# Moving normalisation, a branch and several sums of a stick-breaking / convolution layer between stages and queues

## The chip, the cores and the metric

The kernel runs on one core of a Trainium2 chip. The core has a matrix engine (PE, with its weight loads shown apart as PEld), a vector engine (DVE), an activation engine (ACT), a general engine (POOL) and a queue engine (SP); transfers run on 16 DMA engines. Each engine works through its own instructions in order. The metric is the device time of the program in microseconds (us).

## What is computed

The input is x, 2048 positions of 1024 numbers. After a layer normalisation one product with `w_in` gives nine blocks; two branches follow and are merged:

```python
h = layer_norm(x) @ w_in                     # q k v z_sb c_val c_gate z_cv g_sb g_cv
o_sb = stick_breaking_attention(q, k, v)     # 16 heads of 64
y_sb = (o_sb * silu(z_sb)) @ w_sb_proj
u = causal_depthwise_conv(c_val * sigmoid(c_gate))        # 31 taps
u = silu(layer_norm(u, conv_ln_g, conv_ln_b))
y_cv = (u * silu(z_cv)) @ w_cv_proj
merged = sigmoid(g_sb) * y_sb + sigmoid(g_cv) * y_cv
out = layer_norm(2 ** 0.25 * layer_norm(x) + merged @ w_out)
# attention, s < t: weight(t, s) = sigmoid(l_ts) * prod over s < j < t of (1 - sigmoid(l_tj))
```

Everything is in 32-bit floating point.

## The kernel before

**Numbers split in two.** A matrix operand is kept as a high part `hi` (a rounded copy, made on ACT) and a low part `lo = src - hi` (DVE); a product is three matmuls, hi x hi, hi x lo, lo x hi. `split` (lines 115 to 117) does this, for activations, weights and attention weights alike. So L116 is ACT and L117 is DVE wherever something is split.

**Tiles and stages.** The positions run backwards in memory and are cut in four chunks of 512; chunks 3 and 2 form half h = 1, chunks 1 and 0 half h = 0. Channels are eight blocks of 128. What is needed later goes to DRAM tiles (`asb` attention's output, `acv` the convolution branch's, `mdr` the merged product, `gat` the gates, `vtd` v) and comes back as 128x512 tiles `st`, of which there are seven.

*First phase* (`first_phase`, matmuls on line 909, 0 to about 1193 us). 56 groups of two column blocks of `w_in`, each as seven products (a Strassen-like scheme), 14 pieces of six matmuls each. 36 groups are for h = 1 (all blocks), 20 for h = 0 (convolution input "u", and the gates c, g, h). `order(h)` gives the order: eight u groups with the rest spread evenly between them. A group's results go to a use function: `silu_to` for z and c (sigmoid on ACT, line 320, then a multiplication on DVE, line 321), `sig_to` for g and h.

*Attention stage* (to about 2740 us). `weave_attention` puts the steps of 16 heads in an order, and the pieces of a list F ("fill": plain products on line 201, six matmuls a piece) are spread evenly between them by position in the list. For a step: logits (two matmuls, lines 583 and 584), a sigmoid on ACT (586), a running product along the row by a DVE scan (589), transposes on PE (612), a split on ACT and DVE, four products with v (628). When a 128-row pair is through, `done` (637 to 650) adds the two 64-row halves of PSUM (ACT copies one, DVE adds the other, line 642), adds v (648), multiplies by the gate (649) and stores to `asb`. The fill before: q, k, v and z for h = 0, then the s branch (attention's output through `w_sb`) of h = 1, then the c branch (`w_cv`) of h = 1. `branch` makes these: the product times its gate (line 712), for c also plus the stored result of s (`pdr`, line 714). `END` entries of the list are left for after the attention.

*Last stage*: s branch of h = 0, output rows of chunks 3 and 2, c branch of h = 0, output rows of chunks 1 and 0 (line 1243).

**The convolution** runs on DVE as 46 multiply-adds (line 409) a block and half, 16 in all. `slow_step` is called after each piece and gives at most one step; `PACES` says by how much a counter rises with each call, for the first half of the first phase, its second half, and the attention stage. These steps have low priority.

**Its normalisation**: `conv_mean` and `conv_ln(c)`: per chunk eight steps `s2` (subtract the mean, line 467, square, sum, 474) and eight steps `s3` (lines 499 to 506: scale, 501, swish by sigmoid and a multiplication, 504, gate, 505), 34 or 28 list entries with empty ones between. Those of h = 1 are delayed into the attention stage's fill from pair `I0` = 1 on; those of h = 0 come after the s branch, every `N1`-th entry.

**Weights.** `load_w` loads a block in two halves (raw, 256 KB) and splits it; where the first phase has stored a split copy (`wdr`), it loads that. The block for the next product is ordered at the second of eight pieces of the present one.

**Order.** PE's instructions stand in the order of the program. Those of the other engines and queues are put in order when the program is built, by priority. All DMAs before are issued on SP.

## Time and profile before

| | before |
|---|---|
| median of 3 runs | 3145.14 us (3144.13 to 3145.33) |
| the profiled execution | 3146.49 us |
| its span, first to last instruction | 3144.7 us |
| granted TensorE clock, mean | 0.978 |
| busy PE / DVE / ACT / POOL | 2896.8 / 2603.8 / 1414.0 / 75.4 us |
| DMA | 605 MB, 192 GB/s over the span |

Rows of the profile name a line of the kernel, an engine, an operation, `out<-in` by the names of the tiles with buffer numbers left out, shapes and a count; then busy time and mean duration, and after the second bar the idle time of the engine just before and what ended it. A matmul's time is longer than the distance to the next one, since matmuls are pipelined. "A <- B: t, n, m" in a list of waits is: A waited for B t us in all, n times, m at the longest. DMA rows give the size and the median time from issue to landing.

### The profile page before, as it was taken

Reading aid. Unit: us, or ns where it says so; the run is one execution under the profiler, and the core shown is the slowest. Engines: PE = TensorE matmul, PEld = TensorE weight load, DVE = VectorE, ACT = ScalarE, POOL = GpSimd, SP = SyncE. Lnnn points to the kernel's source line nnn. Section 1 sums busy time; section 2 is a strip of 40 time slices with the busy share of each in tenths; the row PEclk is TensorE's granted clock in tenths of the full one; section 3 lists DMA queues with packets and bytes.
Section 4 is the critical chain, followed back from the end, with each engine's and each line's share of the span. In section 5 each row is a group of like instructions: output and inputs, shape, how many; then the busy total and the mean of one; then the engine's idle time right before and its main releaser. Section 6 shows DMA issues by size and latency. Waiting matters only on the chain.

```text
span 3144.7 us, 42164 instructions
## 1 busy us (share of the span) xinstructions
PE 2896.8 (92%) x14666; PEld 2402.7 (76%) x14666; DVE 2603.8 (83%) x3537; ACT 1414.0 (45%) x2582; POOL 75.4 (2%) x162
## 2 busy tenths in 40 slices
PE   6998999999999998899889889998899888879998
PEld 4776787878788886787777778887788777767887
DVE  8988989888777865998999988888988898856746
ACT  6553444444422323444454554555645555543322
POOL 1000000000000000000000000000000000000000
PEclk8999999999999999999999999999999999989999
DMA  5878757577865567555563454444543553486552
GB/s 179 301 232 307 264 194 267 206 264 282 286 222 185 176 228 218 169 182 176 182 185 119 149 172 134 156 146 140 167 129 118 158 180 120 145 288 231 169 187 81
DMA packets 319269, 604.98 MB, mean 192 GB/s; under 512 B 37456, under 2 KB 79568, under 8 KB 318928
## 3 DMA queue, kind: packets, MB, share of 16 engines
q1 hardware_dynamic: 319056, 602.29, 58.3%
q8 instruction: 115, 1.88, 0.3%
q14 instruction: 98, 0.80, 0.1%
HBM read 355.74 MB, written 246.42 MB: 191 GB/s over the span
## 4 chain that ended last, share of the span: by engine, by line
PE 47%; DVE 25%; issue 12%; DMA 7%; ACT 3%; SPq 1%; POOL 1%; DVEq 0%; POOLq 0%; ACTq 0%
PE pb L909 11%; PE mm L201 10%; DVE nb L589 10%; PE pp L909 7%; PE mm L909 7%; DVE tl L117 4%; PE tp L612 4%; PE pv L628 3%; PE lg L583 1%; DVE cy L409 1%; PE lg L584 1%; ACT th L116 1%; DVE cu L409 1%; ACT nb L586 1%; DMA st<-fdr 1%
## 5 line engine op out<-in xcount | busy, mean ns | idle before, releaser
L116 ACT ACTIVATE th<-tp 128x512 fp32r<-128x512 f32 (+1 forms) x576 | 329.6, 573 | 467.8 <-PE tp L612 459.2
L117 DVE TENSOR_TENSOR tl<-tp,th 128x512 fp32r<-128x512 f32 (+1 forms) x576 | 374.2, 652 | 92.2 <-ACT th L116 89.1
L612 PE MATMUL tp<-ident,nb 128*128 128x128 f32 x2176 | 354.6, 279 | 80.4 <-DVE nb L589 63.5
L586 ACT ACTIVATE nb<-lg 128x512 f32<-128x512 f32 (+3 forms) x640 | 331.3, 532 | 115.7 <-PE lg L584 114.0
L589 DVE TENSOR_TENSOR_SCAN nb<-nb,dd 128x256 f32<-128x256 f32 (+7 forms) x256 | 343.8, 1348 | 18.0 <-ACT nb L586 18.0
L628 PE MATMUL pv<-tl,v 128*128 128x256 f32 (+1 forms) x1152 | 303.1, 292 | 53.2 <-DVE tl L117 52.5
L612 PEld LDWEIGHTS tp<-ident,nb 128*128 128x128 f32 x2176 | 255.2, 142 | 116.7 <-DVE nb L589 78.8
L589 DVE TENSOR_TENSOR_SCAN nb<-nb,zero 128x1024 f32<-128x1024 f32 x128 | 300.1, 2347 | 23.3 <-ACT nb L586 23.1
L628 PE MATMUL pv<-th,v 128*128 128x256 f32 (+1 forms) x1152 | 307.8, 285 | 2.8 <-ACT th L116 2.6
L583 PE MATMUL lg<-k,qd 128*128 128x512 f32 (+3 forms) x640 | 267.9, 420 | 23.7 <-ACT nb L586 11.7
L628 PEld LDWEIGHTS pv<-tl,v 128*128 128x128 f32 x1152 | 219.1, 190 | 91.7 <-DVE tl L117 76.4
L628 PEld LDWEIGHTS pv<-th,v 128*128 128x128 f32 x1152 | 219.7, 191 | 20.5 <-ACT th L116 4.5
L584 PE MATMUL lg<-k,ql 128*128 128x512 f32 (+3 forms) x640 | 234.7, 367 | 0.0
L201 PE MATMUL mm<-A11h,w 128*128 128x512 f32 x512 | 185.6, 409 | 12.7 <-ACT w L116 7.0
L409 DVE SCALAR_TENSOR_TENSOR cy<-cu,csum,cy 128x512 f32<-128x512 f32 x240 | 179.2, 747 | 18.9 <-ACT cy L405 15.8
L201 PE MATMUL mm<-A12h,w 128*128 128x512 f32 x512 | 188.0, 413 | 0.0
L201 PE MATMUL mm<-SXh,w 128*128 128x512 f32 x512 | 182.8, 403 | 2.1 <-DVE st L712 2.1
L201 PE MATMUL mm<-A22h,w 128*128 128x512 f32 x512 | 182.7, 403 | 0.0
L409 DVE SCALAR_TENSOR_TENSOR cu<-cd,cwt,cu 128x512 f32<-128x512 f32 x240 | 179.1, 746 | 3.7
L409 DVE SCALAR_TENSOR_TENSOR cy<-cu,cwt,cy 128x512 f32<-128x512 f32 x240 | 179.1, 746 | 2.6
L583 PEld LDWEIGHTS lg<-k,qd 128*128 128x128 f32 x640 | 122.5, 191 | 48.7 <-ACT nb L586 29.0
L584 PEld LDWEIGHTS lg<-k,ql 128*128 128x128 f32 x640 | 123.7, 193 | 8.8 <-issue 0.2
(251 smaller groups left out, 6298.9 us busy)
## 6 DMA issues: line engine op xcount, KB each, us to landing
wdr<-w4x SPq DMA_DIRECT2D x78, 512.0 KB, 3.4
wdr<-w SPq DMA_DIRECT2D x68, 512.0 KB, 3.2
w4x<-wdr SPq DMA_DIRECT2D x52, 512.0 KB, 4.7
wraw<-in_w_in SPq DMA_DIRECT2D x100, 256.0 KB, 3.5
w<-wdr SPq DMA_DIRECT2D x96, 256.0 KB, 3.8
k<-kdr SPq DMA_DIRECT2D x192, 128.0 KB, 3.0
v<-vdr SPq DMA_DIRECT2D x96, 256.0 KB, 3.0
w<-wdr SPq DMA_DIRECT2D x46, 512.0 KB, 4.4
```

The source lines that it names most:

```text
L116: nc.scalar.activation(hi, src, AF.Copy)
L117: nc.vector.tensor_tensor(out=lo, in0=src, in1=hi.bitcast(F32), op=ALU.subtract)
L201: nc.tensor.matmul(box["ps"], lhsT=l[:, kb], rhs=r[kb], start=(kb == 0 and n == 0), stop=(kb == KB - 1 and n == 2))
L409: nc.vector.scalar_tensor_tensor(out=dst, in0=src[:, j:j + HN], scalar=t, in1=first, op0=ALU.mult, op1=ALU.add)
L583: nc.tensor.matmul(lg[:, :w], lhsT=qd[c][:, js], rhs=k2[kc][:, ko:ko + w], start=True, stop=False)
L584: nc.tensor.matmul(lg[:, :w], lhsT=ql[c][:, js], rhs=k2[kc][:, ko:ko + w], start=False, stop=True)
L586: nc.scalar.activation(nb[:, o:o + w], lg[:, :w], AF.Sigmoid, scale=-QS)
L589: nc.vector.tensor_tensor_scan(out=nb[:, :w], data0=nb[:, :w], data1=dd[:, :w] if diag else zero.to_broadcast([P, w]), initial=0.0 if diag ...
L612: nc.tensor.transpose(out=tp[:, at_:at_ + P], in_=tiles[j][:, so:so + P], identity=ident)
L628: nc.tensor.matmul(o[:, :w], lhsT=lv, rhs=tt[:, o0:o0 + w], start=(diag and t == 0 and n == 0 and e == 0), stop=(last and t == nt - 1 and ...
L909: nc.tensor.matmul(bank, lhsT=wt[:, e, kb], rhs=xs_[kb][a], start=start and kb == 0 and n == 0, stop=kb == 3 and n == 2, skip_group_check= ...
```

## The change

- `order`: the u groups come after every third other group (h = 1) or every one (h = 0), what remains at the end.
- Swish of z and c in the first phase as one activation (`AF.Silu`) from PSUM; in the attention stage z stays as it was.
- The normalisation of h = 1 starts in the first phase, at group `NORM` = 45, every second entry. That of h = 0 starts with the s branch of h = 1 instead of after it and goes one entry at a time (`N1` 2 to 1).
- The c branch of h = 0 joins the attention stage's fill, ahead of the s branch of h = 0; `END` is 24. The last stage is the s branch of h = 0 and all the outputs.
- Sums by accumulating DMA, issued on POOL: the second branch's result into `mdr` (no `pdr`), the two halves of attention's output and v into its tile (ACT copies the second half), and the low part of a weight (ACT writes -hi, the DMA adds the raw block from DRAM). Splits of `w_sb` and `w_cv` are stored and loaded again for h = 0.
- `PACES`, second entry: 1.25 to 1.6.

```diff
-PACES = [0.78, 1.25, 0.6]
-I0 = 1
+PACES = [0.78, 1.6, 0.6]
+NORM = 45
-END = 14
+END = 24
-N1 = 2
+N1 = 1
...
             nc.sync.dma_start(out=raw, in_=src[col // P][:, ks])
-            split(raw, hi[:, ks], lo[:, ks])
+            nc.scalar.activation(hi[:, ks], raw, AF.Copy)
+            nc.scalar.activation(lo[:, ks], hi[:, ks].bitcast(F32), AF.Copy, scale=-1.0)
+            nc.gpsimd.dma_start(out=lo[:, ks], in_=src[col // P][:, ks].bitcast(F32R), accum_op=ALU.add)
+            if src is not w_in:
+                d = wdr[id(src), col, g] = dram([P, 2, 4, P], F32R, f"wdr{len(wdr)}b")
+                dma(d[:, 0], hi[:, ks])
+                dma(d[:, 1], lo[:, ks])
...
-    def sig_to(i, e):
+    def gate_to(i, e, func):
         def use(c, ps):
             s = st()
-            nc.scalar.activation(s, ps, AF.Sigmoid)
+            nc.scalar.activation(s, ps, func)
...
             nc.scalar.activation(s[hs], ps[ls], AF.Copy)
-            nc.vector.tensor_tensor(out=g[hs], in0=ps[hs], in1=s[hs], op=ALU.add)
+            nc.scalar.activation(g[hs], ps[hs], AF.Copy)
+            nc.gpsimd.dma_start(out=g[hs], in_=s[hs], accum_op=ALU.add)
             if a == 0:
                 return
-            v, z = st(), st()
-            dma(v, vtd[c, i])
+            z = st()
+            nc.gpsimd.dma_start(out=g, in_=vtd[c, i], accum_op=ALU.add)
             dma(z, gat[c, i, "b"])
-            nc.vector.tensor_tensor(out=g, in0=g, in1=v, op=ALU.add)
             nc.vector.tensor_tensor(out=g, in0=g, in1=z, op=ALU.mult)
...
-            def use(c, ps, g, *a):
+            def use(c, ps, g):
                 o = st()
                 nc.vector.tensor_tensor(out=o, in0=ps, in1=g, op=ALU.mult)
-                for a_ in a:
-                    nc.vector.tensor_tensor(out=o, in0=o, in1=a_, op=ALU.add)
-                dma((mdr if a else pdr)[c, m], o)
+                if n == "sc"[h == 0]:
+                    dma(mdr[c, m], o)
+                else:
+                    nc.gpsimd.dma_start(out=mdr[c, m], in_=o, accum_op=ALU.add)
...
-                    g["uses"] = [(silu_to if e in "zc" else sig_to)(n, blocks[e][1]) for n in i]
+                    g["uses"] = [gate_to(n, blocks[e][1], AF.Silu if e in "zc" else AF.Sigmoid) for n in i]
...
+            n = 3 if h else 1
             out_ = []
-            for n, u in enumerate(us_):
-                out_.append(u)
-                out_ += rest[len(rest) * n // 8:len(rest) * (n + 1) // 8]
-            return out_
+            for m in range(KB):
+                out_ += [("u", m)] + rest[m * n:m * n + n]
+            return out_ + rest[KB * n:]
...
+            if n == NORM:
+                F.soon([(0.1, it) for it in conv_mean(1) + conv_ln(3) + conv_ln(2)], 1, 2)
...
         F.pair(gate_z(NPAIR - 2), gate_z(NPAIR - 1), freed=loads("s", 1))
-        F.soon([(0.1, it) for it in norm], 1, 2)
+        F.soon([(0.1, it) for it in conv_mean(0) + conv_ln(1) + conv_ln(0)], N0, N1)
         run(F, branch("s", 1), loads("c", 1))
-        F.soon([(0.1, it) for it in conv_mean(0) + conv_ln(1) + conv_ln(0)], N0, N1)
-        run(F, branch("c", 1), loads("s", 0))
+        run(F, branch("c", 1), loads("c", 0))
+        run(F, branch("c", 0), loads("s", 0))
...
         run(F, branch("s", 0), loads("m", 1))
-        output(F, 3, loads("c", 0)[0])
-        output(F, 2, loads("c", 0)[1])
-        run(F, branch("c", 0), loads("m", 0))
+        output(F, 3, loads("m", 0)[0])
+        output(F, 2, loads("m", 0)[1])
         output(F, 1, ())
         output(F, 0, ())
```

More of the change, by code (lines that the diff above doesn't have):

```diff
@@ L99, in layer_kernel @@
     mdr = {(c, m): dram([P, CH], F32, f"mdr{c}_{m}") for c, m in CM}
-    pdr = {(c, m): dram([P, CH], F32, f"pdr{c}_{m}") for c, m in CM}
     qdr = {(c, m): dram([2, P, CH], F32R, f"qdr{c}_{m}") for c, m in CM}
@@ L700, in gate @@
             return load
-        def other(m):
-            def load(c):
-                a = st()
-                dma(a, pdr[c, m])
-                return a
-            return load
         def use(m):
-            def use(c, ps, g, *a):
+            def use(c, ps, g):
                 o = st()
                 nc.vector.tensor_tensor(out=o, in0=ps, in1=g, op=ALU.mult)
-                for a_ in a:
-                    nc.vector.tensor_tensor(out=o, in0=o, in1=a_, op=ALU.add)
-                dma((mdr if a else pdr)[c, m], o)
-            return use
-        src, bys = (w_sb, [gate]) if n == "s" else (w_cv, [gate, other])
-        return [(src, m * P, [(c, lambda c=c: acts[n, c]) for c in half(h)], use(m)) + tuple(b(m) for b in bys)
+                if n == "sc"[h == 0]:
+                    dma(mdr[c, m], o)
+                else:
+                    nc.gpsimd.dma_start(out=mdr[c, m], in_=o, accum_op=ALU.add)
+            return use
+        return [(w_sb if n == "s" else w_cv, m * P, [(c, lambda c=c: acts[n, c]) for c in half(h)], use(m), gate(m))
                 for m in range(KB)]
@@ L999, in order @@
         def order(h):
-            us_ = [("u", m) for m in range(KB)]
             rest = [(e, m) for m in range(4) for e in ("kqvzcgh" if h else "cgh")]
+            n = 3 if h else 1
             out_ = []
-            for n, u in enumerate(us_):
-                out_.append(u)
-                out_ += rest[len(rest) * n // 8:len(rest) * (n + 1) // 8]
-            return out_
+            for m in range(KB):
+                out_ += [("u", m)] + rest[m * n:m * n + n]
+            return out_ + rest[KB * n:]
         groups = [group(1, *o) for o in order(1)] + [group(0, *o) for o in order(0)]
@@ L1159, in layer_kernel @@
             ready[1, i] = True
-        norm = conv_mean(1) + conv_ln(3) + conv_ln(2)
         for i in range(NPAIR):
@@ L1164, in layer_kernel @@
                 F.block(*gate_z(i))
-            for q in range(10):
-                if norm and i >= I0:
-                    F.delay(1 + 3 * q, 0.1, norm.pop(0))
         F.pair(gate_z(NPAIR - 2), gate_z(NPAIR - 1), freed=loads("s", 1))
-        F.soon([(0.1, it) for it in norm], 1, 2)
+        F.soon([(0.1, it) for it in conv_mean(0) + conv_ln(1) + conv_ln(0)], N0, N1)
         run(F, branch("s", 1), loads("c", 1))
-        F.soon([(0.1, it) for it in conv_mean(0) + conv_ln(1) + conv_ln(0)], N0, N1)
-        run(F, branch("c", 1), loads("s", 0))
+        run(F, branch("c", 1), loads("c", 0))
+        run(F, branch("c", 0), loads("s", 0))
         end = len(F.pieces) - END
```

## The prediction

> **What bounds the kernel now.** I read the chain of waits first, because busy shares are averages over stages that differ.
>
> ```profile
> PE 47%; DVE 25%; issue 12%; DMA 7%; ACT 3%; SPq 1%; POOL 1%; DVEq 0%; POOLq 0%; ACTq 0%
> ```
>
> The chain that ended last runs through PE, and for a quarter of its length through DVE. Next I cut the span where the kind of matmul changes (the last L909 at 1193 us, the last attention matmul near 2740 us). The columns are span, PE, PE weight load, DVE, ACT and POOL busy, each with its instructions, then the granted clock, the DMA share and GB/s.
>
> ```profile
> 0.00:1196.00 1196.00, 1135.66 (x4930) 917.60 (x4930) 997.21 (x1554) 486.03 (x862) 40.87 (x87) 0.98 0.70 239
> 1196.00:2735.00 1539.00, 1381.85 (x8115) 1177.73 (x8116) 1348.14 (x1590) 798.34 (x1542) 16.62 (x27) 0.98 0.50 157
> 2735.00:3145.00 410.00, 379.25 (x1623) 307.40 (x1621) 258.45 (x394) 129.61 (x179) 17.90 (x48) 0.96 0.57 188
> ```
>
> The first phase is PE's (95% busy). In the attention stage PE shows 90% and DVE 88%. In the last stage PE shows 92% and DVE 63%. But a matmul's shown duration overlaps the next one's, so what PE needs is counted from start to start:
>
> ```profile
> 2107.17 0.60 PE L612 MATMUL tp<-ident,nb 128*128 128x128 f32 x4
> 2107.52 0.47 PE L583 MATMUL lg<-k,qd 128*128 128x512 f32 x1
> ...
> 2108.06 0.28 PE L628 MATMUL pv<-th,v 128*128 128x256 f32 x1
> ...
> 2108.53 0.39 PE L201 MATMUL mm<-A11h,w 128*128 128x512 f32 x1
> ...
> 2109.91 0.60 PE L612 MATMUL tp<-ident,nb 128*128 128x128 f32 x4
> ```
>
> Four transposes take 0.35 us, a 512-wide pair of logits 0.54, four pv 0.47, six fill matmuls 1.38 (0.230 each). A 512-wide matmul where nothing waits takes 120/524 = 0.229 us (below, 960:1080). The stage's counts are 2268 fill matmuls (L201, below), and from the page 2176 transposes, 2304 pv and 640 logit pairs (435 columns on average by the code, so about 0.47 us). 2268 x 0.229 + 2176 x 0.088 + 2304 x 0.117 + 640 x 0.47 = 1281 us, 83% of 1539. So the attention stage is filled by neither engine; its DVE is the fuller one. Windows of 80 us show how the two share it:
>
> ```profile
> 240.00:320.00 80.00, 69.16 (x279) 54.83 (x280) 66.53 (x104) 26.56 (x47) 0.12 (x1) 0.94 0.85 289
> 480.00:560.00 80.00, 78.36 (x350) 63.86 (x349) 73.49 (x117) 34.10 (x62) 4.38 (x8) 1.00 0.78 281
> 720.00:800.00 80.00, 76.70 (x326) 61.91 (x325) 64.80 (x100) 34.73 (x59) 0.00 (x0) 0.98 0.89 313
> ...
> 1280.00:1360.00 80.00, 70.67 (x398) 60.24 (x399) 76.25 (x104) 37.16 (x77) 0.19 (x1) 0.94 0.46 147
> 1920.00:2000.00 80.00, 74.10 (x444) 63.57 (x443) 63.50 (x71) 40.69 (x80) 1.04 (x1) 1.00 0.54 165
> 2320.00:2400.00 80.00, 79.33 (x467) 68.29 (x466) 62.09 (x70) 38.51 (x73) 0.00 (x0) 1.00 0.43 135
> 2640.00:2720.00 80.00, 67.86 (x388) 56.88 (x387) 71.37 (x84) 44.26 (x82) 0.00 (x0) 0.96 0.42 142
> ```
>
> For the 18 windows from 1280 to 2720 I counted PE's need in the same way (64.4 us in the first, 77.0 in 2320:2400, 59.4 in the last) and fitted 80 = a x PE need + b x DVE busy: a = 0.57, b = 0.59, with a scatter of some 2 us a window. A us taken from DVE gives back about 0.59 us, a us of PE work put in costs about 0.57. This is an estimate; I use it for the stage.
>
> **The change part by part.** The attention stage first; its DVE rows (stage window, mean ns, idle before):
>
> ```profile
> L642 DVE TENSOR_TENSOR og<-pv,st 64x512 f32<-64x512 f32 x63 | 42.9, 681 | 4.4 <-ACT st L641 3.4
> ...
> L117 DVE TENSOR_TENSOR w<-wraw,w 128x512 fp32r<-128x512 f32 x48 | 32.1, 682 | 7.1 <-PE tp L612 3.3 <-ACT w L116 2.9 <-PE lg L584 1.0
> ...
> L648 DVE TENSOR_TENSOR og<-og,st 128x512 f32<-128x512 f32 x31 | 21.1, 679 | 3.4 <-DMA st<-vtd 3.4
> L712 DVE TENSOR_TENSOR st<-mm,gt 128x512 f32<-128x512 f32 x30 | 20.5, 682 | 5.2 <-PE mm L201 5.1
> L505 DVE TENSOR_TENSOR st<-st 128x512 f32<-128x512 f32 x24 | 16.8, 699 | 0.2
> L504 DVE TENSOR_TENSOR st<-st 128x512 f32<-128x512 f32 x24 | 16.4, 684 | 0.9 <-ACT st L503 0.9
> L501 DVE TENSOR_TENSOR st<-st,mu 128x512 f32<-128x512 f32 x24 | 16.4, 682 | 3.4 <-DMA st<-ydq 3.3
> L467 DVE TENSOR_TENSOR st<-st,mu 128x512 f32<-128x512 f32 x24 | 16.2, 679 | 1.3 <-DMA st<-ydr 1.2
> L474 DVE TENSOR_TENSOR sum<-sum,st 128x512 f32<-128x512 f32 x21 | 14.3, 683 | 0.9 <-ACT st L469 0.7
> ...
> L714 DVE TENSOR_TENSOR st<-st 128x512 f32<-128x512 f32 x14 | 9.6, 686 | 0.2
> ```
>
> The halves and v go to accumulating DMAs: -42.9 - 21.1. The low parts of the weights likewise: -32.1. L714's adds: -9.6. Normalising: 24 of each of five lines run here now (chunks 3, 2 and 1; chunk 0's 8 come in the last stage). Then it is chunks 1 and 0, 16 of each: -8 x (0.679 + 0.683 + 0.682 + 0.684 + 0.699) = -27.4. The half-0 conv branch moves in. END counts entries of the list, moved loads among them: the last 14 now hold 6 pieces (a piece is six matmuls), the last 24 then hold 12. So L712 goes from 30 to 48 - 3 = 45, +10.2, and the splits of what it reads add some 11 x 0.684 = +7.5. Sum -115 us of DVE. PE:
>
> ```profile
> 1196.00:2735.00 1539.00, 610.90 (x2268) 416.17 (x2268) 0.98 0.50 157
> 2735.00:3145.00 410.00, 193.60 (x804) 156.59 (x804) 0.96 0.57 188
> ```
>
> That is L201. 64 pieces come, 6 more stay behind: +58 x 6 = 348 matmuls x 0.229 = +79.7 us. Stage: 0.57 x 79.7 - 0.59 x 115 = **-23 us**; with 2 us a window either way (19 windows) -60 to +15.
>
> What I cost at nothing there: ACT gains 63 copies of a half (0.59 us) and 48 negated copies (0.63), 67 us, against 741 us in which it has nothing to do; if that cover fails, at most those 67. POOL is busy 17 us of 1539 and takes some 160 accumulating DMAs (64 halves, 32 v, 48 weights, 16 of c's results). Their duration stands in no row. The nearest are SP's 256 KB transfers, fastest and slowest:
>
> ```profile
> st<-vtd SPq DMA_DIRECT2D x32, 256.0 KB, 3.1
> asb<-og SPq DMA_DIRECT2D x32, 256.0 KB, 2.0
> ...
> wraw<-in_w_sb SPq DMA_DIRECT2D x32, 256.0 KB, 4.2
> ...
> st<-gat_0b SPq DMA_DIRECT2D x4, 256.0 KB, 6.3
> ```
>
> I take 3 us, bounds 2.0 and 6.3. A weight block then needs 4.2 + 2 x 0.63 + 6.3 = 11.8 us at worst; it is ordered six pieces ahead, and 1539 us hold 378 pieces, 24 us of lead. In the last stage the weights come ready-split from DRAM. SP's write of lo waits behind the accumulation, so whatever is queued on SP behind it (heads' q, k, v) is up to 6.3 us later, 32 times; those have several buffers, so nothing. The chained sums are a rival below.
>
> The convolution does not move.
>
> ```profile
> 1196.00:2735.00 1539.00, 101.70 (x138) 0.98 0.50 157
> ```
>
> That is L409. A call of slow_step does at most one step however large the pace is, so 1.25 and 1.6 give the same. Counting steps and pieces leaves three and a bit convolutions for the attention stage in both orders; 3 x 46 taps = 138. Cost nothing, bounds 5 us either way (the order of the groups).
>
> **First phase.** Chunks 3 and 2 are normalised here from group 45 of 56 on, about 970 us:
>
> ```profile
> 960.00:1080.00 120.00, 120.00 (x524) 98.00 (x523) 96.21 (x140) 36.01 (x61) 0.00 (x0) 1.00 0.57 183
> 1080.00:1196.00 116.00, 112.13 (x485) 90.54 (x483) 69.58 (x99) 23.54 (x39) 2.97 (x6) 1.00 0.71 230
> ```
>
> DVE: 165.8 us of 236 now, +16 x 3.43 = +55, -8 swish multiplications (0.687 by the row below) = 215, 91%. At 92%, in 480:560, PE was still 98% busy. The 80 transfers of 256 KB that come along are 21 MB, +89 GB/s on about 206. At 281 to 313 GB/s windows lost 1.6 and 3.3 us of 80, at 289 (240:320) 10.8. Over three such windows I take **+8 us**, bounds 0 and 32.
>
> ```profile
> L944 ACT ACTIVATE gt<-pp 128x512 f32<-128x512 f32 x56 | 33.5, 598 | 104.0 <-PE pp L909 104.0
> ...
> L321 DVE TENSOR_TENSOR st<-mm,st 128x512 f32<-128x512 f32 x28 | 19.2, 687 | 9.2 <-ACT st L320 9.0
> ```
>
> One activation for the swish: 48 multiplications (32 for h = 1, 16 for h = 0) x 0.687 = 33 us off a DVE that does not set the time. Nothing; the other end is a rival.
>
> **Last stage.** 348 matmuls fewer, -79.7. Of its stalls go PE's waits for the normalisation's sum and for the split of w_sb:
>
> ```profile
> PE mm L201 <- ACT w L116: 7.0, 2, 6.2
> ...
> PE mm L483 <- DVE sum L474: 5.8, 1, 5.8
> ```
>
> -12.8; whether the freed time is lost to the loads of s0 instead is the bound (0). Together **-93**, bounds -80 to -105.
>
> Sum: +8 - 23 - 93 = -108. The profiled execution took 3146.5 us (span 3144.7, 1.8 around it), 1.4 over the median. 3146.5 - 108 = 3038.5 by its own time, 3037 by the median's; I say **3038**. Own range, from the bounds: 2980 to 3105.
>
> **The rivals.**
>
> *DVE's relief frees PE altogether.* In 2320:2400, with DVE at 62 of 80, PE's need was 77.0 of 80. If all the stage ran so: (1281 + 80) x 80/77.0 = 1414, -125 instead of -23: 2936. Against it: DVE would still be at 1233 of 1414, 87%, where that window had 78%. 0.07.
>
> *The stage stays as it is.* In 1920:2000 DVE had 63.5 us to a PE need of 70.3, a ratio of 0.90, the ratio that 1233 to 1361 will have. At that filling 1361 x 80/70.3 = 1549, +10: 3071. For it: it is the nearest mixture; against it: one window. 0.20.
>
> *Switching functions on ACT.* By the order of the groups, swish and sigmoid follow one another some 18 times in the first phase. If the engine needs time to change over, PSUM is drained later. In the row above the copy L944 waited 104 us for PE over 56 copies: 1.9 us to spare each time, so a change-over of an activation's length (0.6) is hidden. If it took twice what there is to spare, 18 x 1.9 = +34: 3072. 0.08. The Trainium skill, ScalarE: Activation LUTs, "What ACT_TABLE_LOAD costs", gives about 2.66 us for every switch to another set of tables; by it, if the two functions are in different sets, it would be 18 x 0.76 = +14, 3052; no run here shows a switch.
>
> *Slower: the multiplication by the gate holds up DVE.* In the rows above L648 waited 3.4 us in all for its load, as DVE's order fits the landing. Then L649 waits for two accumulations into the same tile, one after the other, and DVE takes its queue in order: tl, whose lateness already shows on PE, stands behind it. If the order allows for one landing (3.1 us) and the two take 6.3 each, 9.5 us x 32 = 304 us x 0.59 = +179: 3217. It decides from 108/(0.59 x 32) = 5.7 us a time. For it: no row shows how long an accumulation takes; against it: rows of 2 to 4 us are the rule. 0.10. The Trainium skill, DMA: Bandwidth & Descriptors, "Rules for kernel authors", says that an accumulation beside another access of the same bytes loses a write and must wait for the earlier semaphore; that is the series assumed here, which no trace yet shows.
>
> **How the numbers follow.** Forecast 0.55, the rivals 0.07, 0.20, 0.08 and 0.10. The range runs from 2970 to 3108: below it lies most of the first rival, above it the slower one. A measurement of this kernel tells 0.2% (6 us) from no change. Slower: 0.09, most of the last rival; within 0.2%: 0.03, the path to it; faster: 0.88.
>
> **What would show it.** Attention's last matmul about 23 us earlier after a first phase 8 us longer; DVE there about 1233 us; no L642, L648 and L714; L201 in the last stage about 456; the accumulations' landing times; whether L649 waits for DMA; ACT idle between swish and sigmoid; L409 still about 138 times in the attention stage. I am wrong if DVE falls and the stage does not follow, or if DVE waits for the accumulations.

## The result, and the profile after

The changed kernel takes **3258.95 us** (median of 4 executions, 3255.87 to 3270.73) against 3144.64 us of the kernel before (3142.41 to 3145.33): a ratio of **1.0372, interval 1.0345 to 1.0398**. It is slower by 114 us where 107 us less was forecast. The profiled execution, 3270.73 us, is the slowest of the four. One execution further below, of late_norm, took 4694.07 us at a granted clock of 0.56 and is left out of its ratio.

The first rows of the profile after: busy time of the engines, and then the chain that ended last.

```profile
span 3268.6 us, 42365 instructions
...
PE 2933.2 (90%) x14666; PEld 2439.3 (75%) x14666; DVE 2457.9 (75%) x3281; ACT 1483.7 (45%) x2680; POOL 229.6 (7%) x338
...
PE 16%; issue 16%; DVE 5%; DMA 5%; ACT 2%; POOL 1%; SPq 0%; POOLq 0%; DVEq 0%; ACTq 0%
```

DVE has 146 us less to do, as intended, and the span is 124 us longer all the same. So the loss is in waiting, not in work; the totals can't say where. Cut at the last matmul of the first phase (now L907) and the last of the attention (now L633), with the columns as in the prediction:

```profile
0.00:1265.10 1265.10, 1154.89 (x4965) 932.05 (x4966) 1021.75 (x1591) 545.96 (x930) 43.65 (x87) 0.96 0.71 243
1265.10:2958.90 1693.80, 1488.20 (x8472) 1273.25 (x8471) 1255.63 (x1421) 853.42 (x1642) 152.96 (x186) 0.95 0.60 166
2958.90:3268.60 309.70, 290.12 (x1233) 233.98 (x1231) 180.54 (x269) 84.29 (x108) 32.98 (x65) 0.97 0.55 171
```

Cut at the same matmuls, the kernel before has 1192.5, 1548.5 and 403.7 us. So the first phase is 72.6 us longer, the attention stage 145.3 us longer, and the last stage 94.0 us shorter. In the attention stage PE now shows 88% (90% before) and DVE 74% (87% before).

**The first phase.** Windows of 80 us in which the moved normalisation runs:

```profile
960.00:1040.00 80.00, 68.02 (x274) 53.54 (x273) 54.18 (x83) 25.19 (x42) 1.42 (x1) 0.91 0.62 195
1040.00:1120.00 80.00, 56.08 (x224) 44.54 (x222) 52.72 (x79) 28.41 (x42) 0.00 (x0) 0.85 0.84 274
1120.00:1200.00 80.00, 62.73 (x253) 50.86 (x254) 67.39 (x104) 33.63 (x51) 1.02 (x1) 0.83 0.57 188
```

The first of these windows in the kernel before:

```profile
960.00:1040.00 80.00, 80.00 (x349) 65.15 (x348) 58.34 (x85) 20.68 (x36) 0.00 (x0) 1.00 0.67 215
```

Before, a full window held 349 matmuls; here it is 274, 224 and 253, while DVE has 52.7 to 67.4 us of 80. No engine is full. The timeline of ACT in the second window shows what happens (start, duration, line, tiles; in brackets the idle time before, and what ended it):

```profile
1074.72 0.81 ACT L507 ACTIVATE st<-st,vec 128x512 f32<-128x512 f32 x1 [4.11 <-DVE st L506]
1075.56 0.81 ACT L508 ACTIVATE st<-st,vec 128x512 f32<-128x512 f32 x1
1080.59 0.81 ACT L507 ACTIVATE st<-st,vec 128x512 f32<-128x512 f32 x1 [4.21 <-DVE st L506]
1081.31 0.58 ACT L333 ACTIVATE st<-pb 128x512 f32<-128x512 f32 x1
1081.79 0.80 ACT L508 ACTIVATE st<-st,vec 128x512 f32<-128x512 f32 x1
1086.47 0.81 ACT L507 ACTIVATE st<-st,vec 128x512 f32<-128x512 f32 x1 [3.88 <-DVE st L506]
1087.19 0.58 ACT L948 ACTIVATE st<-pb 128x512 f32<-128x512 f32 x1
```

And PE's timeline at the same place:

```profile
1071.71 0.39 PE L907 MATMUL pp<-S4h,w4x 128*128 128x512 f32 x1
1087.82 0.79 PE L907 MATMUL pb<-S3h,w4x 128*128 128x512 f32 x1 [15.71 <-ACT st L948]
```

PE's next product writes into the PSUM bank that L948 has to copy out first. L948 takes 0.58 us, but ACT executes in order, and three steps of the normalisation (L507, sigmoid; L508, scale) stand ahead of it, each about 6 us after the other because each waits for a DVE operation (L506), which waits for a load of its own. PE stands still for 15.7 us. What comes after is slow too; the same view of the clock, in windows of 3 us:

```profile
1088.00:1091.00 3.00, 3.00 (x8) 2.32 (x9) 2.99 (x5) 1.10 (x2) 0.00 (x0) 0.50 0.44 158
1091.00:1094.00 3.00, 3.00 (x12) 2.44 (x11) 3.00 (x6) 0.06 (x1) 0.00 (x0) 0.80 0.74 225
1094.00:1097.00 3.00, 3.00 (x14) 2.46 (x14) 2.27 (x4) 1.16 (x2) 0.00 (x0) 1.00 0.91 279
```

The granted clock is 0.50 just after the stop and full only some 6 us later (8, 12, then 14 matmuls in 3 us): a stop of PE costs more than its own length. The Trainium skill, TensorE: Matmul & The Clock Gate, Part 1, has a clock of one half after an idle window of about 3.4 us; this row agrees.

PE's longest waits from 960 us to the end of the phase:

```profile
PE pb L907 <- ACT st L948: 35.8, 4, 15.7
PE mm L488 <- DVE sum L479: 10.5, 2, 5.4
PE mm L452 <- DMA st<-ysd: 5.8, 1, 5.8
```

The kernel before has one wait of 0.8 us there. The first row is the copy L948; the other two are small matmuls of the normalisation itself, which stand in PE's queue until their sums or loads are there. From 960 us to the end of the phase PE is idle 54.0 us (0.8 before) and busy 251.15 us (231.72 before), at a granted clock of 0.89 (1.00 before). So of the 72.6 us, 53 are PE standing still and 19 are its matmuls at a lower clock and the normalisation's own.

**The attention stage.** The row of the gate's multiplication, now L654 (L649 before), and that of the products with v that wait for DVE's splits `tl`, now L633 (L628 before); first after, then before:

```profile
L654 DVE TENSOR_TENSOR og<-og,st 128x512 f32<-128x512 f32 x32 | 22.1, 692 | 112.9 <-DMA og<-vtd 64.2 <-issue 48.7
L633 PE MATMUL pv<-tl,v 128*128 128x256 f32 (+1 forms) x1152 | 308.3, 295 | 86.5 <-DVE tl L116 86.1
```

```profile
L649 DVE TENSOR_TENSOR og<-og,st 128x512 f32<-128x512 f32 x32 | 21.8, 682 | 0.4 <-DMA st<-gat_0b 0.2
L628 PE MATMUL pv<-tl,v 128*128 128x256 f32 (+1 forms) x1152 | 303.1, 292 | 53.2 <-DVE tl L117 52.5
```

DVE stands idle for 112.9 us ahead of 32 multiplications, 3.5 us a time (0.4 us in all before), and PE waits 86.1 us for the splits (52.5 before). One of them on the timelines of POOL and then of DVE:

```profile
1516.16 0.79 POOL L648 DMA_DIRECT2D og<-st  x1 [7.48 <-ACT og L647]
1521.88 0.90 POOL L652 DMA_DIRECT2D og<-vtd  x1 [4.93 <-DMA og<-st]
```

```profile
1521.54 0.55 DVE L116 TENSOR_TENSOR tl<-tp,th 128x384 fp32r<-128x384 f32 x1
1527.05 0.69 DVE L654 TENSOR_TENSOR og<-og,st 128x512 f32<-128x512 f32 x1 [4.96 <-issue]
1527.66 0.42 DVE L594 TENSOR_TENSOR_SCAN nb<-nb,dd 128x128 f32<-128x128 f32 x1
1527.99 1.26 DVE L116 TENSOR_TENSOR tl<-tp,th 128x512 fp32r<-128x512 f32 x2
```

The halves' accumulation (L648) must land before v's (L652) is issued, and that one before the multiplication; behind it in DVE's queue stand the scan and the two splits that PE's transposes and pv wait for. The two landings follow from the issue rows (size, median time from issue to landing):

```profile
og<-st POOLq DMA_DIRECT2D x64, 128.0 KB, 4.0
og<-vtd POOLq DMA_DIRECT2D x32, 256.0 KB, 4.4
mdr<-st POOLq DMA_DIRECT2D x32, 256.0 KB, 6.0
...
w<-in_w_cv POOLq DMA_DIRECT2D x16, 256.0 KB, 7.6
```

### The profile page after: what moved, and what is told of

It reads as the page before. It is cut to its first block, busy times and chain, and to the rows that moved or that the text cites. A ratio compares the mean times of both kernels' runs of the same rounds, so it can differ in the third digit from the quotient of the medians.

```text
span 3268.6 us, 42365 instructions
## 1 busy us (share of the span) xinstructions
PE 2933.2 (90%) x14666; PEld 2439.3 (75%) x14666; DVE 2457.9 (75%) x3281; ACT 1483.7 (45%) x2680; POOL 229.6 (7%) x338
## 5 line engine op out<-in xcount | busy, mean ns | idle before, releaser
L633 PE MATMUL pv<-tl,v 128*128 128x256 f32 (+1 forms) x1152 | 308.3, 295 | 86.5 <-DVE tl L116 86.1
L594 DVE TENSOR_TENSOR_SCAN nb<-nb,dd 128x256 f32<-128x256 f32 (+7 forms) x256 | 344.3, 1350 | 31.3 <-ACT nb L591 30.4
L617 PEld LDWEIGHTS tp<-ident,nb 128*128 128x128 f32 x2176 | 262.8, 145 | 109.8 <-DVE nb L594 73.7
L594 DVE TENSOR_TENSOR_SCAN nb<-nb,zero 128x1024 f32<-128x1024 f32 x128 | 299.8, 2347 | 32.3 <-ACT nb L591 32.1
L633 PE MATMUL pv<-th,v 128*128 128x256 f32 (+1 forms) x1152 | 312.3, 290 | 3.5 <-ACT th L115 3.4
L633 PEld LDWEIGHTS pv<-tl,v 128*128 128x128 f32 x1152 | 225.8, 196 | 119.4 <-DVE tl L116 103.7
L588 PE MATMUL lg<-k,qd 128*128 128x512 f32 (+3 forms) x640 | 267.0, 418 | 26.7 <-ACT nb L591 15.7
L633 PEld LDWEIGHTS pv<-th,v 128*128 128x128 f32 x1152 | 225.4, 196 | 21.4 <-ACT th L115 5.7
L206 PE MATMUL mm<-A11h,w 128*128 128x512 f32 x512 | 189.9, 415 | 9.9 <-DMA w<-wdr48b 5.0
L206 PE MATMUL mm<-SXh,w 128*128 128x512 f32 x512 | 189.1, 414 | 0.0
L206 PE MATMUL mm<-A12h,w 128*128 128x512 f32 x512 | 188.8, 413 | 0.0
L206 PE MATMUL mm<-A22h,w 128*128 128x512 f32 x512 | 187.9, 411 | 0.0
L588 PEld LDWEIGHTS lg<-k,qd 128*128 128x128 f32 x640 | 125.0, 195 | 52.1 <-ACT nb L591 29.7
L589 PEld LDWEIGHTS lg<-k,ql 128*128 128x128 f32 x640 | 125.7, 196 | 11.6
```

What stands on the lines that cost most here:

```text
L206: nc.tensor.matmul(box["ps"], lhsT=l[:, kb], rhs=r[kb], start=(kb == 0 and n == 0), stop=(kb == KB - 1 and n == 2))
L588: nc.tensor.matmul(lg[:, :w], lhsT=qd[c][:, js], rhs=k2[kc][:, ko:ko + w], start=True, stop=False)
L589: nc.tensor.matmul(lg[:, :w], lhsT=ql[c][:, js], rhs=k2[kc][:, ko:ko + w], start=False, stop=True)
L594: nc.vector.tensor_tensor_scan(out=nb[:, :w], data0=nb[:, :w], data1=dd[:, :w] if diag else zero.to_broadcast([P, w]), initial=0.0 if diag ...
L617: nc.tensor.transpose(out=tp[:, at_:at_ + P], in_=tiles[j][:, so:so + P], identity=ident)
L633: nc.tensor.matmul(o[:, :w], lhsT=lv, rhs=tt[:, o0:o0 + w], start=(diag and t == 0 and n == 0 and e == 0), stop=(last and t == nt - 1 and ...
```

## The experiments

My theory after this reading: three separate things. The reordering cost about what was forecast; the moved normalisation made the first phase's loss through ACT's queue; the accumulations made the attention's through DVE's. The rivals: the first phase lost to the swish or to the order of the groups; the attention simply paid for the moved matmuls; POOL's queue delays the weights. The table has the stages of each one's profiled execution, cut as above, and the ratio of times to the kernel before, which was measured again beside each group of runs (medians of 3144 to 3148 us).

| kernel | first phase | attention | last | median us | ratio to before |
|---|---|---|---|---|---|
| before | 1192.5 | 1548.5 | 403.7 | 3144.64 | |
| changed | 1265.1 | 1693.8 | 309.7 | 3258.95 | 1.0372 (1.0345 to 1.0398) |
| u_done | 1269.6 | 1611.6 | 307.8 | 3180.44 | 1.0116 (1.0080 to 1.0153) |
| u_norm | 1191.6 | 1735.9 | 309.7 | 3234.09 | 1.0281 (1.0247 to 1.0316) |
| u_w | 1274.6 | 1670.1 | 310.5 | 3251.99 | 1.0329 (1.0286 to 1.0372) |
| branch_only | 1191.7 | 1642.3 | 302.3 | 3130.57 | 0.9946 (0.9928 to 0.9964) |
| few_mm | 1186.7 | 1585.5 | 298.4 | 3085.82 | 0.9804 (0.9778 to 0.9831) |
| u_done_norm_w | 1192.8 | 1634.8 | 305.4 | 3135.28 | 0.9971 (0.9960 to 0.9983) |
| late_gate | 1262.1 | 1578.0 | 309.0 | 3164.48 | 1.0068 (1.0048 to 1.0088) |
| norm_skew | 1258.0 | 1679.6 | 310.2 | 3256.65 | 1.0352 (1.0333 to 1.0372) |
| late_even | 1244.6 | 1582.9 | 310.1 | 3136.09 | 0.9968 (0.9954 to 0.9982) |
| late_norm | 1194.2 | 1636.8 | 308.0 | 3140.68 | 0.9982 (0.9967 to 0.9998) |
| late_norm_w | 1193.7 | 1600.9 | 309.4 | 3107.74 | 0.9889 (0.9870 to 0.9909) |
| late_even_w | 1242.4 | 1572.3 | 310.2 | 3121.06 | 0.9933 (0.9913 to 0.9952) |
| ring8 | 1239.4 | 1583.7 | 307.2 | 3133.79 | 0.9967 (0.9949 to 0.9984) |
| half_norm_w | 1228.4 | 1587.2 | 309.5 | 3125.82 | 0.9945 (0.9931 to 0.9960) |

A stage is that of one execution, and profiled executions lay up to 14 us from their kernel's median (late_gate's 14 us under it, the changed kernel's 12 us over it). So I take a difference of stages as good to some 15 us, to 25 us between those two, and give that of the medians beside it.

### Undoing one part of the change

**u_done: the output's sums on VectorE again.**

```diff
-            nc.scalar.activation(g[hs], ps[hs], AF.Copy)
-            nc.gpsimd.dma_start(out=g[hs], in_=s[hs], accum_op=ALU.add)
+            nc.vector.tensor_tensor(out=g[hs], in0=ps[hs], in1=s[hs], op=ALU.add)
...
-            nc.gpsimd.dma_start(out=g, in_=vtd[c, i], accum_op=ALU.add)
+            dma(v, vtd[c, i])
+            nc.vector.tensor_tensor(out=g, in0=g, in1=v, op=ALU.add)
```

> The changed kernel with the halves of the attention's output and v added on VectorE again (v loaded by SP), the rest as changed. Theory A (the gate's multiplication L654 stands at the head of VectorE's queue for two accumulations in series, 112.9 us of VectorE idle, and TensorE waits behind it): this wait falls to a few us, VectorE's work grows by some 64 us (32 x 1.34 and 32 x 0.66), and the attention stage of 1694 us becomes 1580 to 1630; the time 3259 becomes 3145 to 3195. Theory B (the stage is long because TensorE has 80 us more to do in it and the weights come through POOL's queue): the stage stays within 20 us of 1694, the time within 20 us of 3259. The first phase (1265) and the last stage (310) stay by both.

The attention fell by 82 us, the median by 79. The groups of lines of u_done, its L654:

```profile
L654 DVE TENSOR_TENSOR og<-og,st 128x512 f32<-128x512 f32 x32 | 21.9, 683 | 0.7 <-DMA st<-gat_1b 0.4
```

And its attention stage in the view of windows:

```profile
1269.60:2881.20 1611.60, 1463.21 (x8472) 1252.85 (x8471) 1312.38 (x1515) 820.95 (x1579) 76.09 (x92) 0.97 0.57 170
```

The wait is gone, and the stage is shorter although DVE has 57 us more to do in it (1312.38 against 1255.63). Theory A. It does not yet say whether the wait or something else about the accumulations costs.

**u_norm: the normalisation of chunks 3 and 2 back in the attention.**

```diff
-            if n == NORM:
-                F.soon([(0.1, it) for it in conv_mean(1) + conv_ln(3) + conv_ln(2)], 1, 2)
...
+            for q in range(10):
+                if norm and i >= 1:
+                    F.delay(1 + 3 * q, 0.1, norm.pop(0))
```

> The changed kernel with the normalisation of chunks 3 and 2 back among the attention's filling pieces, as before the change, the rest as changed. Theory A (the normalisation in the first phase holds ScalarE's queue, and TensorE's next product waits for ScalarE's copy at L948): the first phase's end falls from 1265 to 1190 to 1205, the attention stage grows by 27.4 us of VectorE's work at 0.59, some 16 us, and the time is about 3205 (3190 to 3220). Theory B (the first phase was lost to the swish's table loads or to the order of its groups): the first phase stays at 1250 or more and the time is 3259 to 3285.

The first phase ends at 1191.6, 0.9 us from that of the kernel before, though the swish, the new order of groups and the pace 1.6 are still in it: all of its loss is the moved normalisation. But the attention grew by 42 us instead of 16, so the median fell by 25 us only, to 3234 us, above the 3190 to 3220 expected. The 16 us priced 8 steps of each line, the net of the whole change; this edit puts back 16 (chunks 3 and 2), and DVE has 47 us more in the stage (1302.96 against 1255.63), 28 us by the same price.

**u_w: the low parts of the weights on VectorE.**

```diff
-            nc.scalar.activation(hi[:, ks], raw, AF.Copy)
-            nc.scalar.activation(lo[:, ks], hi[:, ks].bitcast(F32), AF.Copy, scale=-1.0)
-            nc.gpsimd.dma_start(out=lo[:, ks], in_=src[col // P][:, ks].bitcast(F32R), accum_op=ALU.add)
+            split(raw, hi[:, ks], lo[:, ks])
```

> The changed kernel with the low parts of the weights split on VectorE again instead of accumulated through POOL's queue (the store of both parts for the second use stays), the rest as changed. Theory A (the accumulations of weights are early enough to cost nothing): VectorE's work grows by some 32 us, the attention stage by up to 19 us, the time is 3259 to 3280. Theory B (the weights stand in POOL's queue behind the accumulations of L648 and L652, which wait, and come late to TensorE): the stage falls by 20 us or more, the time to 3240 or less.

The attention fell by 24 us, as in theory B, but the median, 3251.99, lies between the two theories, 7 us under the changed kernel's, and the intervals overlap: inconclusive by itself. It was tried again below.

**branch_only: the reordering alone** (the edits of u_done, u_norm and u_w, and sigmoid and `pdr` as before).

> Only the reordering of the change: the second branch of chunks 1 and 0 moved from the last stage into the attention (END 24, N1 1), the order of the first phase's groups and the pace 1.6; no accumulating DMA, sigmoid with VectorE's multiplication instead of the swish, the normalisation of chunks 3 and 2 in the attention as before. Theory A (accumulation waits and the moved normalisation made the loss): the first phase ends at 1190 to 1200, the attention stage is 1547 + 0.57 x 79.7 + 0.59 x 10 = about 1598 (1580 to 1620), the last stage 310 (some 310 to 320), and the time 3100 (3080 to 3130), faster than the kernel before. Theory B (the moved matmuls themselves lengthen the attention one for one, and more by its fuller queues): the stage is 1630 to 1700 and the time 3140 to 3210.

The reordering alone is **faster than the kernel before**, 0.9946, by less than theory A had: the attention has 1642.3 us where it gave 1580 to 1620 and theory B began at 1630. The first phase came as expected; the last stage, 302.3, is 8 us shorter than the 310 to 320 expected.

**u_done_norm_w: the reordering with the swish and the branches' accumulation.**

> The reordering with the swish as one activation in the first phase and the accumulation of the branches' sum in DRAM (POOL), but with the output of the attention and the low parts of weights on VectorE and the normalisation of chunks 3 and 2 in the attention. Theory A (these two parts cost nothing and take 9.6 us off VectorE in the attention and some 60 off it in the first phase): the first phase ends within 5 us of 1192, the attention stage is 1630 to 1642, the time 3118 to 3132. Theory B (ScalarE's switches between the tables of swish and sigmoid, or the accumulation, cost something): 3140 or more.

First phase and attention are 1192.8 and 1634.8, as theory A had it; the median, 3135.28, lies 5 us above branch_only's, between the two. The switches do happen (ACT's groups by form, in this kernel; one more load stands elsewhere, and the kernel before has two in all):

```profile
L331 ACT ACT_TABLE_LOAD x13 | 16.7, 1283 | 11.8 <-PE mm L905 9.5 <-DMA wraw<-in_w_in 2.1
L358 ACT ACT_TABLE_LOAD x6 | 7.7, 1283 | 0.1
```

Swish and sigmoid are in different tables: 1.283 us a load. In the first phase ACT is busy 546 of 1265 us in the changed kernel, and the loads are hidden.

### Where the accumulations cost

**late_gate: both accumulations kept, only the multiplication moved down DVE's queue.**

```diff
+LATE = 14
...
-            z = st()
-            dma(z, gat[c, i, "b"])
-            nc.vector.tensor_tensor(out=g, in0=g, in1=z, op=ALU.mult)
-            dma(asb[c, i], g)
+            def gated():
+                z = st()
+                dma(z, gat[c, i, "b"])
+                with tc.issue_after(newest()):
+                    nc.vector.tensor_tensor(out=g, in0=g, in1=z, op=ALU.mult)
+                dma(asb[c, i], g)
+            late.append([LATE, gated])
...
             fn()
+            for e in list(late):
+                e[0] -= 1
+                if e[0] < 0:
+                    late.remove(e)
+                    e[1]()
```

> The changed kernel with both accumulations of each output kept, but VectorE's multiplication by the gate set some ten instructions further down its queue (fourteen of the attention's items later). Theory A (the head of VectorE's queue, waiting for the second accumulation, is what makes the 82 us of the accumulated output): the idle time ahead of the multiplication falls from 112.9 us to under 30 and the attention stage from 1694 to about 1610 to 1640, the time to 3175 to 3205. Theory B (the cost lies elsewhere: in POOL's queue, in ScalarE's extra copy, in the tiles held longer): the wait goes, but the stage stays above 1665 and the time above 3230.

This decides between the two theories. The group of the multiplication, and the attention's window, in late_gate:

```profile
L658 DVE TENSOR_TENSOR og<-og,st 128x512 f32<-128x512 f32 x32 | 21.9, 683 | 13.7 <-DMA st<-gat_0b 3.1 <-DMA og<-vtd 3.0 <-DMA qd<-qdr 2.0
```

```profile
1262.10:2840.10 1578.00, 1449.74 (x8471) 1243.89 (x8470) 1253.36 (x1421) 852.75 (x1642) 153.02 (x186) 0.98 0.65 179
```

The same engines have the same work (DVE 1253 against 1256 us, ACT 853, POOL 153), and the stage is 116 us shorter, the median 94 us. Idle time ahead of the multiplication went from 112.9 to 13.7 us: 99 us of DVE's standing still were worth 94 (medians) to 116 us, about **one for one**, more than theory A had (1610 to 1640 for the stage, 3175 to 3205). On PE's side the 116 us are 77 us less of standing still (205.6 to 128.3) and 38 us less for the same matmuls (1488.20 to 1449.74), at a granted clock of 0.98 in place of 0.95; its wait for `tl` in these products fell from 86.1 to 30.5 us. And the stage is 34 us shorter than u_done's, the median 16 us: once nothing waits, the accumulations do relieve DVE. (The load of the gate is issued later too, by the same edit, and no run separates the two; but in the changed kernel the time ahead of the multiplication was put down to v's accumulation and to issue, not to the gate's load.)

**late_norm, late_norm_w and late_even_w: the weights again, with the queue mended.** late_norm is late_gate with u_norm's edit, late_norm_w has u_w's as well; late_even_w is late_even (below) with u_w's.

> The changed kernel with the gate's multiplication later and the normalisation of chunks 3 and 2 back in the attention. If the parts add up: first phase 1192, attention 1578 + 42 (what the normalisation cost it between the two kernels without the later multiplication) = 1620, last 309, the time 3120 to 3130. If the attention has room again, now that VectorE's queue no longer stands still: attention 1578 to 1595, time 3080 to 3105.

> As the kernel before it in this list, and the low parts of the weights split on VectorE again. Theory A (the 24 us that the weights' accumulations cost the attention came from standing in POOL's queue behind waiting accumulations): 15 to 25 us less than with them. Theory B (that loss too came from VectorE's queue standing still, which is mended): VectorE's 32 us more cost 0 to 20 us.

> The first kernel of this list with the low parts of the weights split on VectorE again. The same two theories: 15 to 25 us less than the first of the list by A, 0 to 20 us more by B.

late_norm kept its stages as the sum had them, with 17 us more in the attention, and came to 3140.68, above either expectation. The weights' accumulations cost 36 and 11 us of the attention, 33 and 15 us of the medians, though DVE has 25 and 26 us more work in the stage without them (1327.05 against 1302.28, 1281.30 against 1255.32). Theory B is out; theory A has the direction, with 33 and 15 us by the medians where 15 to 25 were expected. That POOL's queue is the reason is not shown: no row of PE waits for a late weight. Without them ACT loses 48 negated copies, 29.7 us, and PE's wait for ACT's sigmoid of the logits is halved, 8.5 us of the 36. The lists of waits, late_norm and then late_norm_w:

```profile
PE lg L589 <- ACT nb L592: 17.0, 28, 3.9
```

```profile
PE lg L587 <- ACT nb L590: 8.5, 25, 1.3
```

Which of these it is stays open. late_norm_w is the **fastest of all runs, 3107.74 us, 0.9889**: the reordering, swish, the branches' sum and the output's halves and v by accumulation with a late multiplication, the weights and the normalisation as before.

### What the moved matmuls cost

**few_mm: branch_only with a third of the branches' products left out in the attention** (the weights' low part times the activations, for the s and c branches of h = 1 and the c branch of h = 0).

```diff
+                    few = 2 if src is w_cv or src is w_sb and c > 1 else 3
...
-                        for n, (l, r) in enumerate(((wh, xh), (wh, xl), (wl, xh))):
+                        for n, (l, r) in enumerate(((wh, xh), (wh, xl), (wl, xh))[:few]):
```

> The reordering alone, and without the product of the weights' low part in the three branches that lie in the attention stage: 16 of 24 matmuls for each of 48 outputs, 384 matmuls of 0.229 us less, 88 us; all loads, splits and VectorE work stay. Theory A (TensorE's work lengthens the attention stage one for one): the stage falls from 1642 by 80 to 95 us and the time to 3035 to 3055. Theory B (the fit of the prediction, 0.57 us of the stage for each us of TensorE's need): the stage falls by 50 us (45 to 55) and the time to about 3080. If the stage hardly moves (under 30 us), its length is set by the chains between engines.

The attention's windows of branch_only and of few_mm:

```profile
1191.70:2834.00 1642.30, 1477.27 (x8507) 1261.90 (x8506) 1397.02 (x1665) 828.12 (x1583) 26.35 (x30) 0.96 0.56 175
```

```profile
1186.70:2772.00 1585.30, 1395.53 (x8148) 1192.35 (x8147) 1391.11 (x1665) 826.84 (x1583) 26.82 (x30) 0.97 0.58 182
```

PE has 82 us less and the stage 57 us less, the median 45 us: 0.55 to 0.70 us for each us. Theory B, near the fit's 0.57; the moved matmuls are not paid one for one.

### Where the first phase loses its time

**norm_skew: ACT's part of each normalisation step put out one step later.**

```diff
+        def skew(a, b):
+            return [lambda m=m: (a(m) if m < KB else None, b(m - 1) if m else None) for m in range(KB + 1)]
...
-        return ([m1] + wait + [(lambda m=m: s2(m)) for m in range(KB)] + wait + [m2] + wait + [m3]
-                + [(lambda m=m: s3(m)) for m in range(KB)])
+        return [m1] + wait + skew(s2, s2b) + wait + [m2] + wait + [m3] + skew(s3, s3b)
```

> The changed kernel with the moved normalisation still in the first phase, but with ScalarE's part of each of its steps (square; sigmoid and scale) put out one step later than the load and the VectorE operation that it needs. Theory A (ScalarE stands in order at these instructions, 37.4 us at L507 and 13.7 at L474, with TensorE's next product behind its copy L948, 35.8 us): ScalarE's waits fall to 15 us or less and the first phase from 1265 to 1215 to 1235, the time to 3210 to 3230. Theory B (the first phase is long because VectorE and the DMA queues are full with the normalisation): it stays above 1250, the time above 3240.

A miss: 1258.0, and 3256.65. But the edit did not do what it was meant to. Its trace still has four such steps in ACT's queue in the 12 us ahead of the copy (now L958; the sigmoid is L515), and PE waiting for it; from the timeline:

```profile
1071.77 0.81 ACT L515 ACTIVATE st<-st,vec 128x512 f32<-128x512 f32 x1 [2.56 <-DVE st L517]
...
1082.75 0.81 ACT L515 ACTIVATE st<-st,vec 128x512 f32<-128x512 f32 x1
...
1083.50 0.60 ACT L958 ACTIVATE st<-pb 128x512 f32<-128x512 f32 x1
...
1084.15 0.80 PE L917 MATMUL pb<-S3h,w4x 128*128 128x512 f32 x1 [11.86 <-ACT st L958]
```

So it is no evidence for theory B. By the code, the steps stand in bunches because they are set after every second entry of the list, and entries that only load or build weights, which lie together, count too.

**late_even: late_gate with one step after every second matmul piece instead.**

```diff
-                F.soon([(0.1, it) for it in conv_mean(1) + conv_ln(3) + conv_ln(2)], 1, 2)
+                norm += conv_mean(1) + conv_ln(3) + conv_ln(2)
...
-                for q in pc[p]:
+                for k, q in enumerate(pc[p]):
                     F.add(*q)
+                    if norm and k:
+                        F.add(0.1, norm.pop(0))
```

> The changed kernel with the gate's multiplication later (as in the run before) and with the moved normalisation still in the first phase, but one step of it after every second piece of matmuls instead of after every second piece of any kind (pieces that only load or build weights counted too, so that up to five steps of ScalarE's sigmoid and scale stood together ahead of the copy that TensorE waits for). Theory A (these bunches make the first phase's loss): its end falls from 1262 to 1205 to 1230, the attention stage stays at 1570 to 1590, the time 3090 to 3125. Theory B (the normalisation's work and transfers fill VectorE and the queues of the first phase, however spread): the first phase stays above 1250, the time above 3140.

The first phase ends 17.5 us earlier (the medians: 28 us), where 32 to 57 were expected: between the two theories. PE's waits for ACT's copy there fell from 35.7 us (late_gate) to 20.5. Two of its windows:

```profile
1040.00:1120.00 80.00, 70.70 (x295) 56.67 (x294) 59.48 (x91) 40.28 (x55) 1.48 (x1) 0.94 0.80 264
...
1200.00:1280.00 80.00, 54.32 (x249) 43.71 (x248) 56.42 (x78) 34.41 (x59) 4.05 (x7) 0.85 0.78 231
```

In the first of them the changed kernel had 224 matmuls, late_even has 295. Its remaining stops, from the timeline of PE:

```profile
984.93 2.05 PE L453 MATMUL mm<-st,ones 128*128 128x512 f32 x2 [4.08 <-DMA st<-ysd]
...
1180.67 2.05 PE L500 MATMUL mm<-ident,st 128*128 128x128 f32 x8 [3.88 <-DVE st L498]
...
1217.09 0.80 PE L913 MATMUL pb<-S3h,w4x 128*128 128x512 f32 x1 [11.58 <-ACT st L954]
```

One of 11.6 us for ACT's copy is still among them, and two for the normalisation's own small matmuls.

**ring8: one shared tile more. half_norm_w: half of the normalisation, at half the density.**

> The kernel with the later gate's multiplication and the evenly spread normalisation in the first phase, with eight shared tiles (st) in place of seven. Theory A (the steps of the normalisation hold up to three of seven tiles each, and ScalarE's and SP's queues wait for a tile to come free, 28.3 us at ScalarE's sigmoid): the first phase falls from 1245 by 10 us or more. Theory B (the tiles are not what is short): it stays within 5 us of 1245.

> The kernel with the later gate's multiplication and the weights split on VectorE, with the mean of chunks 3 and 2 and the normalisation of chunk 3 alone in the first phase at half the density, and that of chunk 2 in the attention. None of it in the first phase gave 1193.7 and 1600.9, all of it 1242.4 and 1572.3. Theory A (the loss grows with the amount): first phase 1215 to 1222, attention about 1587, the time within 8 us of 3114. Theory B (what costs is the density of the steps; spread wider they fit in): first phase 1195 to 1208, the time 3090 to 3105, the fastest of all. Theory C (a few places where TensorE itself waits, for the means' sums and the like, cost the most, however many steps): first phase 1225 or more.

The shared tiles are not it: 5 us less, and the medians differ by 2. With half of the normalisation in it the first phase ends at 1228.4: 35 us over late_norm_w's 1193.7, where all of it costs 49 (late_even_w). Theory B is out. Theory C's bound (1225) holds, but theory A's upper end lies only 6 us lower, less than a stage is good to. PE's own time from 960 us on says more: it stands still 0.8 us in late_norm_w, 19.2 here and 31.7 in late_even_w, and is busy 16.3 and 17.8 us longer than in late_norm_w. So the standing still fell with the steps, and the longer busy time hardly did; why is not shown.

## Why the prediction was wrong, step by step

**The last stage: right.** -93 was forecast, -94.0 measured, and by the terms of the sum: PE's busy time fell by 83.3 us (79.7 forecast) and its idle time by 10.7 (12.8). L206 runs 462 times in it (about 456 forecast). The convolution's taps in the attention stage stayed at 138, as worked out.

**The first phase: +8 forecast (0 to 32), +72.6 measured.** The step that failed is the one that priced the phase by DVE's filling (91%) and the DMA rate. DVE did not reach it (67.4 us of 80, 84%, at most in the windows above; 213.63 of the 305.10 us from 960 on, 70%), and u_norm shows that the normalisation makes the whole loss. What decides is whose instructions stand in ACT's queue ahead of L948. The prediction listed ACT's idle time (1.9 us a time ahead of L944) as cover for the swish, but never asked what the normalisation's waiting instructions do to it. What the runs showed in its place: PE stands still for 53 us at ACT's copy and at the normalisation's own matmuls, and is 19 us longer busy. An even spread of the steps gave back 17 of the 72.6 us (28 by the medians); no run takes the rest apart.

**The attention stage: -23 forecast (-60 to +15), +145.3 measured.** DVE's work fell by 96 us (115 forecast), and the stage did not follow, the sign of being wrong that the prediction named. The terms of its sum, put together by the edits of the experiments:

| term | forecast | stages | medians |
|---|---|---|---|
| reordering (branch_only) | 0.57 x 79.7 + 0.59 x 45.1 = +72 | +94 | |
| output's halves and v by accumulation | 0.59 x -64.0 = -38 | +82; -34 with the late multiplication | +79; -16 |
| weights' low parts | 0.59 x -32.1 = -19 | +24; +36 and +11 with it | +7; +33 and +15 |
| normalisation of chunks 3 and 2 out of the stage | 0.59 x -54.8 = -32 | -42; -59 with it | |
| swish and branches' sum | 0.59 x -9.6 = -6 | -7.5 | +5 |

(The sum has -27.4 us for the normalisation, the net of 54.8 that leave and 27.4 of chunk 0 that come in; here the 27.4 stand with the reordering, 10.2 + 7.5 + 27.4 = 45.1 us. DVE's work in branch_only's window lies 45.5 us over that of the kernel before, 1397.02 - 1351.46, by this row of the kernel before:

```profile
1192.50:2741.00 1548.50, 1388.06 (x8156) 1182.84 (x8155) 1351.46 (x1595) 801.70 (x1547) 17.62 (x29) 0.98 0.50 157
```

The changes of the medians hold the other stages too, so none is given where those move.) The forecasts add up to -23, the first measured numbers of the stages to about +150, against +145.3. So the parts nearly add, and the accumulated output is the largest miss: +82 where -38 was forecast, 120 of the 168 us between forecast and measurement.

The step that failed is the one that left the wait for the accumulations out of the sum ("The chained sums are a rival below"). That **rival was right in its mechanism and place** (L649, now L654; two accumulations in series; tl behind it) and had a chance of 0.10. Two of its numbers were wrong. A wait was priced at the fit's 0.59, which was fitted on DVE's *busy* time; a stop of DVE with PE's operands behind it cost about 1.0. So the point from which it decides was not 5.7 us a time but 108/32 = 3.4, and the 3.5 us a time that came were enough, 99 us of idle time for 94 to 116 us. And the bounds of an accumulation's landing, 2.0 to 6.3 us, were taken from plain transfers of another engine: the output's two kinds landed within them (4.0 and 4.4 us), the weights' did not (up to 7.6).

A second term that failed is the weights': ACT's negated copies and POOL's work were put at nothing, and 19 us of relief were forecast where the accumulations cost 11 to 36 us. Which of the two costs it stays open.

The fit's price for busy time came near for PE's work (0.55 to 0.70 measured against 0.57) and, once nothing waits, for the output (-16 to -34 against -38); the reordering and the normalisation moved the stage by a third more than it gave (94 against 72, 42 against 32; 59 with the late multiplication).

The other rivals. DVE's relief did not free PE. The stage staying as it is comes nearest to late_gate's 1578.0 (29 over the stage of before, where the rival gave 10 over). Switching of ACT's functions did not show in the time: u_done_norm_w, with the swish and the branches' sum, lies 5 us over branch_only, and its first phase 1.1 us. The Trainium skill, ScalarE: Activation LUTs, "What ACT_TABLE_LOAD costs", gives 2.66 us for every switch; the rows here show 1.283 us for a load, and no run shows the rest.

## What to carry to other kernels

Before an addition is handed from an engine to an accumulating transfer, look for the first instruction that reads the sum: if it stands in an in-order queue ahead of work that another engine waits for, move it down until the transfers have landed, and price its wait at one for one, as it cost here, not at the worth of the engine's busy time. Work that moves into a phase with idle engines still costs what its waiting instructions hold up: space them by the pieces of the engine that bounds the phase. Undo parts one at a time after such a change; here the reordering was a gain of 0.5% hidden under losses of 4%, and with one multiplication moved and two parts undone the same ideas gave 1.1%.

## What the runs showed of the hardware

- An accumulating transfer on POOL's queue took 4.0 us (128 KB) to 7.6 us (256 KB, weights) from issue to landing, and its issue keeps POOL for 0.8 to 1.1 us on average, by kind (0.79 and 0.90 on the timeline above). Two kinds of plain loads of 256 KB by SP, `wraw<-in_w_in` and `v<-vdr`, took 3.5 us at the median in the same kernel.
- A stop of 15.7 us was followed by matmuls at a granted clock of 0.50, full speed coming back after some 6 us.
- Swish and sigmoid in turn gave 20 table loads of 1.283 us in u_done_norm_w, where branch_only, without the swish, has two.
- DVE's own durations were the same beside POOL's transfers: a split took 654 ns (652 before), a scan 1350 (1348).
